# LayerNorm statistics moved off GpSimd, and its transposes placed later, in a two-layer decoder trunk

## The chip, the cores and the metric

The kernel runs on one core of one Trainium2 chip. The metric is the device time of one execution in microseconds (us). Three runs of the kernel before took 904.04, 904.43 and 904.75 us; their median is 904.43 us. The profile comes from a further execution that took 903.08 us.

## The reference

The program is a decoder trunk of two layers over 256 tokens of width 1024, in float32. Each layer has three sublayers: a mixer (three kinds of attention, gated and projected), a cross-attention into a memory of 256 tokens, and a squared-ReLU MLP of width 4096. Behind each stands the update that the change touches:

```python
def layer_norm(x, g, b):
    mu = jnp.mean(x32, axis=-1, keepdims=True)
    var = jnp.mean(jnp.square(x32 - mu), axis=-1, keepdims=True)
    return ((x32 - mu) * lax.rsqrt(var + LN_EPS) * g + b).astype(x.dtype)
...
for l in range(DEPTH):
    y = hybrid_mixer(x, ...)
    x = layer_norm(DN_ALPHA * x + y, ln_g[l, 0], ln_b[l, 0])
    y = memory_cross_attention(x, mem, ...)
    x = layer_norm(DN_ALPHA * x + y, ln_g[l, 1], ln_b[l, 1])
    y = jnp.square(jax.nn.relu(x @ mlp_w_up[l])) @ mlp_w_down[l]
    x = layer_norm(DN_ALPHA * x + y, ln_g[l, 2], ln_b[l, 2])
return x
```

So there are six LayerNorms, each over 256 tokens.

## The kernel before, in words

The 256 tokens are two halves of 128, one token per partition; the residual stream is kept in `xtok` (128 x 2 x 1024). Each LayerNorm is therefore done twice, once per half (`tb` 0 and 1): twelve LayerNorm halves in all. The text names them by place and half: M0 and M1 behind the mixer, X0 and X1 behind the cross-attention, F0 and F1 behind the MLP. In the second layer F0 and F1 end the program and write the output.

Every product is done in three passes, because each float32 operand is split into a high and a low part that TensorE takes at full speed: high times high, high times low, low times high (`mm3`, L322). ScalarE makes the high part of a weight piece (`whi`, or `phi` where it lies in a page; L266) and VectorE the low part (`wlo`, `plo`; L267), in pieces of 128 x 512. The same two engines split the activations: `xhi` (L340) and `xlo` (L341) are the residual stream, transposed, with the channels on the partitions. Weights come from one stream in HBM through a ring of five raw buffers; SyncE issues the load of a buffer once VectorE has taken its last piece from it.

A LayerNorm half works on two column halves. `ln_part` (L450, VectorE) adds the sublayer's product to the residual and sums each row into `mv[:, 0]` or `mv[:, 1]`. `ln_square` (L461, ScalarE) squares the columns, with a bias made of the first sum, and puts the row sums into `mv[:, 2]` and `mv[:, 3]`. The rest are one-column operations (128 x 1) on `mv`: three scaled copies of the first sum (L459), the eps (L463), and in `stats` the mean's remainder (L475), its square (L476), the variance (L477) and the power -0.5 (L478), all on GpSimd, and the mean on VectorE (L479). Two passes of VectorE then make the result: z = (x - mean) * g (L482, tile `lnz`) and x = z * rstd + b (L486). Where a sublayer follows, TensorE transposes the new x in four 128 x 128 pieces per column half (L492) and the two splits follow.

Two things set the order. `Side` queues hold small steps that are put between the big products: a step is issued when so many ticks (about one us of TensorE work each) have gone by, or at once where its result is needed (`need`). For LayerNorm these are `stats`, at once, and `result` twice, one tick apart; `LNW` is the wait of the first. The tile framework then schedules the program on each engine by its own estimates, so that the order on an engine is not simply the order of the code. Each engine takes its instructions strictly in that order.

Of the kernel before, what the change touches and what calls it, by code (L numbers as in the profile page):

```python
# [10 lines left out]
F32 = mybir.dt.float32  # L11
F32R = mybir.dt.float32r
AF = mybir.ActivationFunctionType
OP = mybir.AluOpType
# [4 lines left out]
D = 1024  # L19
L = 2  # L20
P = 128
# [4 lines left out]
ROOT = 32.0  # L26
# [5 lines left out]
WN = 2.0  # L32
WF = 1.5
WARM = 10
LNW = 1
NP = 8
TICK = 1.0
AHEAD = 4
# [191 lines left out]
class Kernel:  # L230
# [223 lines left out]
    def ln_square(self, tb, i):  # L454
        nc, mv = self.nc, self.mv[tb]
        xs = self.xtok[:, tb, 512 * i:512 * i + 512]
        if i == 0:
            for c, k in ((4, -2.0 / (D * ROOT)), (5, 1.0 / D), (6, -1.0 / D)):
                nc.gpsimd.tensor_scalar(mv[:, c:c + 1], mv[:, 0:1], k, None, op0=OP.mult)  # L459
        sq = self.half([P, 512], F32, "lnsq")  # L460
        nc.scalar.activation(sq, xs, AF.Square, bias=mv[:, 4:5], scale=1.0 / ROOT, accum_out=mv[:, 2 + i:3 + i])  # L461
        if i == 0:
            nc.gpsimd.tensor_scalar(mv[:, 7:8], mv[:, 2:3], 1e-5, None, op0=OP.add)  # L463

    def layer_norm(self, tb, gb, final=False):

        nc = self.nc
        x, mv = self.xtok[:, tb, :], self.mv[tb]
        col = [mv[:, i:i + 1] for i in range(12)]
        st = {}  # L470

        def stats():
            z = st["z"] = self.page([P, D], F32, "lnz")

            nc.gpsimd.tensor_scalar(col[8], col[1], -1.0 / D, col[5], op0=OP.mult, op1=OP.add)  # L475
            nc.gpsimd.tensor_scalar(col[9], col[8], col[8], col[7], op0=OP.mult, op1=OP.subtract)  # L476
            nc.gpsimd.tensor_tensor(col[10], col[3], col[9], op=OP.subtract)  # L477
            nc.gpsimd.tensor_tensor(col[11], col[10], self.mhalf, op=OP.pow)  # L478
            nc.vector.tensor_scalar(col[6], col[1], -1.0 / D, col[6], op0=OP.mult, op1=OP.add)  # L479
            for i in range(2):  # L480
                c = slice(512 * i, 512 * i + 512)
                nc.vector.scalar_tensor_tensor(z[:, c], x[:, c], col[6], gb[0][:, c], op0=OP.add, op1=OP.mult)  # L482

        def result(i):
            c = slice(512 * i, 512 * i + 512)
            nc.vector.scalar_tensor_tensor(x[:, c], st["z"][:, c], col[11], gb[1][:, c], op0=OP.mult, op1=OP.add)  # L486
            if final:
                nc.sync.dma_start(self.out[tb * P:(tb + 1) * P, c], x[:, c])
                return
            ps = self.bank("T", [P, 4, P])  # L490
            for k in range(4):
                nc.tensor.transpose(ps[:, k, :], x[:, 512 * i + k * P:512 * i + (k + 1) * P], self.ident)  # L492
            ds = (slice(None), slice(4 * i, 4 * i + 4), slice(tb * P, (tb + 1) * P))
            self.to_hilo(self.xhi[ds], self.xlo[ds], ps)
        tag = ("ln", tb)
        self.side[1].add(stats, 0, tag)
        self.side[1].add(lambda: result(0), LNW, tag)
        self.side[1].add(lambda: result(1), 1, tag)
        self.side[1].tick()

    def ln_done(self, tb):
# [679 lines left out]
```

## Time and profile before

| | |
|---|---|
| median of 3 runs | 904.43 us (904.04 to 904.75) |
| the profiled execution | 903.08 us |
| its span (first to last instruction) | 901.3 us |
| TensorE matmul busy | 877.9 us, 97% of the span, 6034 instructions |
| VectorE busy | 643.7 us, 71% |
| ScalarE busy | 540.9 us, 60% |
| GpSimd busy | 52.8 us, 6%, 114 instructions |
| granted TensorE clock | 0.997 over the span, the 2.4 GHz level |

The 1.8 us between the execution's time and its span lie before the first and behind the last instruction. Names of engines in the rows: PE is TensorE's matmul, PEld its weight load, DVE is VectorE, ACT is ScalarE, POOL is GpSimd, SP is SyncE. `out<-in` names the tiles written and read; a bracket behind a row gives the time for which the engine sat idle before it, and the instruction that ended this.

### The profile page before, as it was taken

The numbers are of one execution on the slowest core, as the hardware profiler recorded it, in microseconds if no ns is written. First come the engines' busy times: TensorE is split into PE (matmuls) and PEld (weight loads), VectorE is DVE, ScalarE is ACT, GpSimd is POOL, SyncE is SP. The second block draws the span as 40 slices with busy tenths as digits, with TensorE's granted clock in tenths as the row PEclk, the third lists the DMA queues.
The fourth block names the chain that finished last, engine by engine and source line by source line (L and its number), as shares of the span: only waits on it lengthen the run. The fifth ranks groups of instructions, "written<-read, shape, count | busy, mean of one in ns | idle before, by whom it ended". The sixth has DMA issues, their size and how long they took to land.

```text
span 901.3 us, 16105 instructions
## 1 busy us (share of the span) xinstructions
PE 877.9 (97%) x6034; PEld 798.0 (89%) x6034; DVE 643.7 (71%) x1411; ACT 540.9 (60%) x1173; POOL 52.8 (6%) x114
## 2 busy tenths in 40 slices
PE   8999999999999999999999999999999999999996
PEld 6999899998877999999889999999988689999994
DVE  5888898768886555555776989886778845555554
ACT  6777967556683444555656777675567545555551
POOL 1000000001211000000130000000021300000002
PEclk9999999999999999999999999999999999999998
DMA  9854645547553566666645435554667446666631
GB/s 330 264 184 146 207 159 158 160 148 275 181 201 118 187 194 192 190 188 190 209 123 179 143 118 178 178 160 139 194 210 252 165 123 187 190 196 188 191 95 47
DMA packets 46539, 160.80 MB, mean 178 GB/s; under 512 B 5941, under 2 KB 7381, under 8 KB 46334
## 3 DMA queue, kind: packets, MB, share of 16 engines
q1 hardware_dynamic: 46462, 159.78, 55.2%
q8 instruction: 47, 0.77, 0.3%
q14 instruction: 30, 0.25, 0.1%
HBM read 158.68 MB, written 1.07 MB: 177 GB/s over the span
## 4 chain that ended last, share of the span: by engine, by line
PE 86%; DVE 5%; POOL 3%; ACT 2%; issue 2%; DMA 1%; DVEq 0%; SPq 0%; POOLq 0%
PE mm L322 51%; PE S L322 14%; PE O L322 10%; DVE wlo L267 1%; PE S L744 1%; PE T L927 1%; POOL mv L476 1%; PE S L1050 1%; DVE xtok L450 1%; DVE xtok L486 1%; PE T L551 1%; PE O L561 1%; DVE xlo L341 1%; PE T L492 1%; DMA raw<-in_wst_dram 1%
## 5 line engine op out<-in xcount | busy, mean ns | idle before, releaser
L267 DVE TENSOR_TENSOR wlo<-raw,whi 128x512 fp32r<-128x512 f32 x524 | 341.0, 687 | 114.1 <-ACT whi L266 110.5
L266 ACT ACTIVATE whi<-raw 128x512 fp32r<-128x512 f32 x524 | 302.2, 624 | 145.1 <-issue 89.3
L322 PE MATMUL mm<-xhi,whi 128*128 128x256 f32 x1024 | 143.9, 282 | 0.1
L322 PE MATMUL mm<-xlo,whi 128*128 128x256 f32 x1024 | 143.8, 281 | 0.0
L322 PE MATMUL mm<-xhi,wlo 128*128 128x256 f32 x1024 | 142.7, 281 | 0.0
L322 PEld LDWEIGHTS mm<-xhi,whi 128*128 128x128 f32 x1024 | 131.8, 188 | 3.7 <-issue 0.7
L322 PEld LDWEIGHTS mm<-xhi,wlo 128*128 128x128 f32 x1024 | 130.4, 188 | 1.6 <-issue 0.3
L322 PEld LDWEIGHTS mm<-xlo,whi 128*128 128x128 f32 x1024 | 130.8, 188 | 1.1
L512 ACT ACTIVATE P<-sb,nm 128x128 f32<-128x128 f32 (+1 forms) x96 | 42.7, 445 | 16.5 <-DVE nm L510 16.1
L322 PE MATMUL S<-whi,hh 128*128 128x512 f32 x128 | 50.4, 394 | 0.0
L322 PE MATMUL S<-wlo,hh 128*128 128x512 f32 x128 | 50.1, 391 | 0.0
L322 PE MATMUL O<-whi,hh 128*128 128x512 f32 x128 | 50.0, 391 | 0.0
L322 PE MATMUL O<-wlo,hh 128*128 128x512 f32 x128 | 49.9, 390 | 0.0
L322 PE MATMUL O<-whi,hl 128*128 128x512 f32 x128 | 49.8, 389 | 0.0
L322 PE MATMUL S<-whi,hl 128*128 128x512 f32 x128 | 49.7, 389 | 0.0
L459 POOL TENSOR_SCALAR mv<-mv 128x1 f32<-128x1 f32 x36 | 9.0, 264 | 672.7 <-DVE xtok L450 671.7
L1125 DVE TENSOR_TENSOR tg<-tg 128x512 f32<-128x512 f32 x28 | 19.4, 692 | 38.4 <-ACT tg L1124 38.4
L1124 ACT ACTIVATE tg<-mm 128x512 f32<-128x512 f32 x28 | 16.7, 597 | 43.2 <-PE mm L322 43.2
L461 ACT ACTIVATE lnsq<-xtok,mv 128x512 f32<-128x512 f32 x24 | 17.3, 721 | 28.5 <-POOL mv L459 15.8
L267 DVE TENSOR_TENSOR plo<-raw,phi 128x512 fp32r<-128x512 f32 x40 | 26.0, 689 | 5.1 <-ACT phi L266 5.0
L322 PEld LDWEIGHTS S<-wlo,hh 128*128 128x128 f32 x128 | 24.0, 188 | 5.6
L322 PEld LDWEIGHTS O<-whi,hl 128*128 128x128 f32 x128 | 24.0, 188 | 5.1
(306 smaller groups left out, 1437.0 us busy)
## 6 DMA issues: line engine op xcount, KB each, us to landing
raw<-in_wst_dram SPq DMA_DIRECT2D x281, 512.0 KB, 3.9
lng<-in_lng_dram SPq DMA_DIRECT2D x6, 512.0 KB, 5.9
lnb<-in_lnb_dram SPq DMA_DIRECT2D x6, 512.0 KB, 5.8
wskew<-bias_scratch SPq DMA_DIRECT2D x4, 400.0 KB, 5.7
xt<-in_xT_dram SPq DMA_DIRECT2D x4, 256.0 KB, 4.1
xtok<-in_xtok_dram SPq DMA_DIRECT2D x1, 1024.0 KB, 6.8
out_dram<-xtok SPq DMA_DIRECT2D x4, 256.0 KB
raw<-in_wst_dram SPq DMA_DIRECT2D x2, 256.0 KB, 4.3
```

What stands on the lines that cost most here:

```text
L266: self.nc.scalar.activation(hi[sl], self.raws[u][sl], AF.Copy)
L267: self.nc.vector.tensor_sub(lo[sl], self.raws[u][sl], r(hi[sl]))
L322: mm(out, a[i], b[j], start=first and ps == 0 and k == 0, stop=last and ps == 2 and k == n - 1)
L341: nc.vector.tensor_sub(lo, src, r(hi))
L450: nc.vector.scalar_tensor_tensor(xs, xs, ALPHA, ac, op0=OP.mult, op1=OP.add, accum_out=mv[:, i:i + 1])
L461: nc.scalar.activation(sq, xs, AF.Square, bias=mv[:, 4:5], scale=1.0 / ROOT, accum_out=mv[:, 2 + i:3 + i])
L476: nc.gpsimd.tensor_scalar(col[9], col[8], col[8], col[7], op0=OP.mult, op1=OP.subtract)
L486: nc.vector.scalar_tensor_tensor(x[:, c], st["z"][:, c], col[11], gb[1][:, c], op0=OP.mult, op1=OP.add)
L492: nc.tensor.transpose(ps[:, k, :], x[:, 512 * i + k * P:512 * i + (k + 1) * P], self.ident)
L512: nc.scalar.activation(p_ap, t[:, :n], AF.Exp, bias=nmax, scale=-1.0, accum_out=sums)
L1124: nc.scalar.activation(t, ps, AF.Relu)
L1125: nc.vector.tensor_mul(t, t, t)
```

## The change

The one-column statistics leave GpSimd, except the power. ScalarE now makes the bias of the square (column 4) and adds the eps (column 7) with two activations in `ln_square`, and the variance (column 10) with a third in `stats`. VectorE makes the two mean columns (5 and 8) straight from both sums, and the square of the mean (9). Per LayerNorm half seven of eight GpSimd operations go, three ScalarE operations come, and VectorE has three one-column operations in place of one.

The transposes become a step of their own, `turn`. The two passes for x are now issued inside `stats`, behind the two passes for z, and `turn(0)` waits three ticks (`LNW` 3 instead of 1), `turn(1)` one more.

```diff
-LNW = 1
+LNW = 3
...
         if i == 0:
-            for c, k in ((4, -2.0 / (D * ROOT)), (5, 1.0 / D), (6, -1.0 / D)):
-                nc.gpsimd.tensor_scalar(mv[:, c:c + 1], mv[:, 0:1], k, None, op0=OP.mult)
+            nc.scalar.activation(mv[:, 4:5], mv[:, 0:1], AF.Copy, scale=-2.0 / (D * ROOT))
         sq = self.half([P, 512], F32, "lnsq")
         nc.scalar.activation(sq, xs, AF.Square, bias=mv[:, 4:5], scale=1.0 / ROOT, accum_out=mv[:, 2 + i:3 + i])
         if i == 0:
-            nc.gpsimd.tensor_scalar(mv[:, 7:8], mv[:, 2:3], 1e-5, None, op0=OP.add)
+            nc.scalar.activation(mv[:, 7:8], mv[:, 2:3], AF.Copy, bias=1e-5)
...
+        def scaled(i):
+            c = slice(512 * i, 512 * i + 512)
+            nc.vector.scalar_tensor_tensor(st["z"][:, c], x[:, c], col[5], gb[0][:, c], op0=OP.add, op1=OP.mult)
+
         def stats():
-            z = st["z"] = self.page([P, D], F32, "lnz")
-
-            nc.gpsimd.tensor_scalar(col[8], col[1], -1.0 / D, col[5], op0=OP.mult, op1=OP.add)
-            nc.gpsimd.tensor_scalar(col[9], col[8], col[8], col[7], op0=OP.mult, op1=OP.subtract)
-            nc.gpsimd.tensor_tensor(col[10], col[3], col[9], op=OP.subtract)
+            st["z"] = self.page([P, D], F32, "lnz")
+
+            nc.vector.tensor_scalar(col[5], col[1], col[0], -1.0 / D, op0=OP.add, op1=OP.mult)
+            nc.vector.tensor_scalar(col[8], col[1], col[0], -1.0 / D, op0=OP.subtract, op1=OP.mult)
+            nc.vector.tensor_scalar(col[9], col[8], col[8], col[7], op0=OP.mult, op1=OP.subtract)
+            nc.scalar.activation(col[10], col[9], AF.Identity, bias=col[3], scale=-1.0)
             nc.gpsimd.tensor_tensor(col[11], col[10], self.mhalf, op=OP.pow)
-            nc.vector.tensor_scalar(col[6], col[1], -1.0 / D, col[6], op0=OP.mult, op1=OP.add)
             for i in range(2):
-                c = slice(512 * i, 512 * i + 512)
-                nc.vector.scalar_tensor_tensor(z[:, c], x[:, c], col[6], gb[0][:, c], op0=OP.add, op1=OP.mult)
+                scaled(i)
+            for i in range(2):
+                result(i)
...
-                return
+
+        def turn(i):
             ps = self.bank("T", [P, 4, P])
...
         self.side[1].add(stats, 0, tag)
-        self.side[1].add(lambda: result(0), LNW, tag)
-        self.side[1].add(lambda: result(1), 1, tag)
+        if not final:
+            self.side[1].add(lambda: turn(0), LNW, tag)
+            self.side[1].add(lambda: turn(1), 1, tag)
```

On TensorE, in the first layer, from the second weight unit of the MLP's first product for half 0 (`mm_3539` before, `mm_3533` in the changed kernel) to the first matmul for half 1 (`mm_3540`, `mm_3534`). The transposes (`T`, L492) are those of X1; `phi` and `plo` are the weights, `xhi` and `xlo` the residual stream. Before:

```order
L322 MATMUL mm_3539<-phi_3326,xhi_92 128x512 x2
L322 MATMUL mm_3539<-phi_3326,xlo_93 128x512 x2
L322 MATMUL mm_3539<-plo_3327,xhi_92 128x512 x2
L322 MATMUL mm_3539<-phi_3434,xhi_92 128x512 x2
L322 MATMUL mm_3539<-phi_3434,xlo_93 128x512 x2
L322 MATMUL mm_3539<-plo_3435,xhi_92 128x512 x2
L322 MATMUL mm_3539<-phi_3494,xhi_92 128x512 x2
L322 MATMUL mm_3539<-phi_3494,xlo_93 128x512 x2
L322 MATMUL mm_3539<-plo_3495,xhi_92 128x512 x2
L492 MATMUL T_3550<-cst_151,xtok_1255 128x128 x4
L492 MATMUL T_3568<-cst_151,xtok_1255 128x128 x4
L322 MATMUL mm_3540<-phi_3291,xhi_92 128x512 x2
```

The same stretch of TensorE in the changed kernel, where the transposes are L497:

```order
L322 MATMUL mm_3533<-phi_3430,xhi_92 128x512 x2
L322 MATMUL mm_3533<-phi_3430,xlo_93 128x512 x2
L322 MATMUL mm_3533<-plo_3431,xhi_92 128x512 x2
L322 MATMUL mm_3533<-phi_3482,xhi_92 128x512
L497 MATMUL T_3561<-cst_151,xtok_1255 128x128 x4
L322 MATMUL mm_3533<-phi_3482,xhi_92 128x512
L497 MATMUL T_3576<-cst_151,xtok_1255 128x128 x4
L322 MATMUL mm_3533<-phi_3482,xlo_93 128x512 x2
L322 MATMUL mm_3533<-plo_3483,xhi_92 128x512 x2
L322 MATMUL mm_3534<-phi_3287,xhi_92 128x512 x2
```

Here the transposes have moved ahead: five of the 24 matmuls for half 0 stand behind the first four transposes and four behind all eight; before, all eight stood behind the 24.

On VectorE, at the same place, from X0's second result (in the changed kernel both results) to the results of X1; the number behind a name is that of its buffer: `lnz` is z, `lnb` and `lng` the LayerNorm's b and g, `mv` the statistics. Before:

```order
L486 SCALAR_TENSOR_TENSOR xtok_1255<-lnz_3474,mv_3442,lnb_3397 128x512
L267 TENSOR_TENSOR plo_3495<-raw_3205,phi_3494 128x512
L341 TENSOR_TENSOR xlo_93<-T_3487,xhi_92 128x4x128
L450 SCALAR_TENSOR_TENSOR xtok_1255,mv_3517<-xtok_1255,S_3482 128x512
L341 TENSOR_TENSOR xlo_93<-T_3504,xhi_92 128x4x128
L450 SCALAR_TENSOR_TENSOR xtok_1255,mv_3517<-xtok_1255,S_3483 128x512
L267 TENSOR_TENSOR wlo_3683<-raw_3513,whi_3682 128x512
L479 TENSOR_SCALAR mv_3517<-mv_3517 128x1
L267 TENSOR_TENSOR wlo_3683<-raw_3513,whi_3682 128x512
L482 SCALAR_TENSOR_TENSOR lnz_3531<-xtok_1255,mv_3517,lng_3395 128x512 x2
L486 SCALAR_TENSOR_TENSOR xtok_1255<-lnz_3531,mv_3517,lnb_3397 128x512 x2
```

The same in the changed kernel, where z is L473 and the result L490:

```order
L490 SCALAR_TENSOR_TENSOR xtok_1255<-lnz_3468,mv_3438,lnb_3393 128x512 x2
L267 TENSOR_TENSOR plo_3483<-raw_3201,phi_3482 128x512
L450 SCALAR_TENSOR_TENSOR xtok_1255,mv_3497<-xtok_1255,S_3478 128x512
L341 TENSOR_TENSOR xlo_93<-T_3506,xhi_92 128x4x128
L450 SCALAR_TENSOR_TENSOR xtok_1255,mv_3497<-xtok_1255,S_3479 128x512
L341 TENSOR_TENSOR xlo_93<-T_3516,xhi_92 128x4x128
L478 TENSOR_SCALAR mv_3497<-mv_3497 128x1
L479 TENSOR_SCALAR mv_3497<-mv_3497 128x1
L473 SCALAR_TENSOR_TENSOR lnz_3523<-xtok_1255,mv_3497,lng_3391 128x512
L480 TENSOR_SCALAR mv_3497<-mv_3497 128x1
L473 SCALAR_TENSOR_TENSOR lnz_3523<-xtok_1255,mv_3497,lng_3391 128x512
L490 SCALAR_TENSOR_TENSOR xtok_1255<-lnz_3523,mv_3497,lnb_3393 128x512 x2
```

The sums of the next half (L450) now each stand one place ahead of a split (`xlo`) where they stood behind it, the two `wlo` splits that stood around the statistics are gone from there, and one of the three one-column operations stands between the two passes for z.

On ScalarE, behind the square of M1's second column half, in the first layer. Before:

```order
L461 ACTIVATE lnsq_3090,mv_2972<-xtok_1255,mv_2972 128x512
L266 ACTIVATE whi_3191<-raw_3014 128x512 x2
L266 ACTIVATE phi_3291<-raw_3075 128x512 x2
L340 ACTIVATE xhi_92<-T_3111 128x4x128
L340 ACTIVATE xhi_92<-T_3131 128x4x128
L1028 ACTIVATE kx_3100<-mm_3101 128x512
```

And in the changed kernel, where L481 is the variance (column 10):

```order
L460 ACTIVATE lnsq_3086,mv_2970<-xtok_1255,mv_2970 128x512
L266 ACTIVATE whi_3187<-raw_3010 128x512 x2
L481 ACTIVATE mv_2970<-mv_2970 128x1
L266 ACTIVATE phi_3287<-raw_3064 128x512 x2
L340 ACTIVATE xhi_92<-T_3132 128x4x128
L1034 ACTIVATE kx_3098<-mm_3099 128x512
L340 ACTIVATE xhi_92<-T_3151 128x4x128
```

The variance stands in ScalarE's queue behind two weight splits.

## Rows read from the trace of the kernel before

**Rows 1.** The page: busy time of TensorE, and the chain that ended last, by engine.

```profile
PE 877.9 (97%) x6034; PEld 798.0 (89%) x6034; DVE 643.7 (71%) x1411; ACT 540.9 (60%) x1173; POOL 52.8 (6%) x114
PE 86%; DVE 5%; POOL 3%; ACT 2%; issue 2%; DMA 1%; DVEq 0%; SPq 0%; POOLq 0%
```

**Rows 2.** What TensorE waited for over the whole span (us in total, times, longest), longest first.

```profile
PE T L492 <- DVE xtok L486: 9.1, 10, 1.4
PE S L322 <- ACT xhi L340: 1.2, 2, 0.7
```

**Rows 3.** All instructions on the statistics tile `mv`, by line: durations in ns (shortest/median/longest), first and last start in us.

```profile
L459 POOL TENSOR_SCALAR mv<-mv x36: 202/208/713, 217.5 to 893.4; 128x1 f32<-128x1 f32 x36
...
L475 POOL TENSOR_SCALAR mv<-mv x12: 261/442/1262, 224.1 to 894.8; 128x1 f32<-128x1 f32 x12
L476 POOL TENSOR_SCALAR mv<-mv x12: 377/1037/1903, 224.5 to 895.5; 128x1 f32<-128x1 f32 x12
...
L478 POOL TENSOR_TENSOR mv<-mv,mhalf x12: 564/568/575, 226.5 to 896.3; 128x1 f32<-128x1 f32 x12
```

**Rows 4.** The timeline at X0 and X1 of the first layer: start us, us, engine, line, operation.

```profile
261.55 0.08 DVE L450 DVE_READ_ACCUMULATOR xtok<-xtok,mm 128x1 f32 x1
...
264.54 0.75 DVE L486 SCALAR_TENSOR_TENSOR xtok<-lnz,mv,lnb 128x512 f32<-128x512 f32 x1 [0.73 <-POOL mv L478]
...
265.44 0.63 PE L492 MATMUL T<-cst,xtok 128*128 128x128 f32 x4 [0.57 <-DVE xtok L486]
...
265.82 0.71 PE L322 MATMUL S<-whi,oxh 128*128 128x512 f32 x2
...
267.07 0.69 DVE L341 TENSOR_TENSOR xlo<-T,xhi 128x512 fp32r<-128x512 f32 x1
...
267.81 0.73 PE L322 MATMUL mm<-phi,xlo 128*128 128x512 f32 x2
...
269.56 0.08 DVE L450 DVE_READ_ACCUMULATOR xtok<-xtok,S 128x1 f32 x1
...
270.43 1.26 POOL L475 TENSOR_SCALAR mv<-mv 128x1 f32<-128x1 f32 x1
...
270.89 1.41 DVE L482 SCALAR_TENSOR_TENSOR lnz<-xtok,mv,lng 128x512 f32<-128x512 f32 x2
...
273.51 1.42 DVE L486 SCALAR_TENSOR_TENSOR xtok<-lnz,mv,lnb 128x512 f32<-128x512 f32 x2 [1.21 <-POOL mv L478]
...
274.41 1.29 PE L492 MATMUL T<-cst,xtok 128*128 128x128 f32 x8 [1.20 <-DVE xtok L486]
...
275.72 0.73 PE L322 MATMUL mm<-phi,xhi 128*128 128x512 f32 x2
```

**Rows 5.** The timeline at the second layer's start: a power on GpSimd (L609, two columns) beside a pair of VectorE splits, and again with VectorE idle.

```profile
460.64 1.29 DVE L267 TENSOR_TENSOR wlo<-raw,whi 128x512 fp32r<-128x512 f32 x2
...
460.82 1.07 POOL L609 TENSOR_TENSOR rs<-ss,mhalf 128x2 f32<-128x2 f32 x1 [4.08 <-DVE ss L608]
...
466.71 0.69 POOL L609 TENSOR_TENSOR rs<-ss,mhalf 128x2 f32<-128x2 f32 x1 [4.83 <-DVE ss L608]
```

**Rows 6.** ScalarE's groups by line and form (count, busy us, mean ns of one), the nearest to a one-column activation, without and with a bias read from a column.

```profile
L837 ACT ACTIVATE kb<-T 128x16 fp32r<-128x16 f32 x4 | 0.7, 171 | 0.0
...
L607 ACT ACTIVATE sq<-S 128x128 f32<-128x128 f32 x4 | 1.1, 272 | 0.0
```

**Rows 7.** The timeline at M0, M1 and in the cross-attention behind them, first layer.

```profile
227.87 0.66 PE L492 MATMUL T<-cst,xtok 128*128 128x128 f32 x4 [0.81 <-DVE xtok L486]
...
233.55 1.15 ACT L266 ACTIVATE whi<-raw 128x512 fp32r<-128x512 f32 x2 [0.61 <-ACT lnsq L461]
...
235.79 1.41 DVE L486 SCALAR_TENSOR_TENSOR xtok<-lnz,mv,lnb 128x512 f32<-128x512 f32 x2 [1.05 <-POOL mv L478]
...
236.68 0.63 PE L492 MATMUL T<-cst,xtok 128*128 128x128 f32 x4 [0.94 <-DVE xtok L486]
...
247.48 1.15 ACT L266 ACTIVATE whi<-raw 128x512 fp32r<-128x512 f32 x2 [0.75 <-DMA raw<-in_wst_dram]
...
248.54 0.46 ACT L537 ACTIVATE P<-S,nm 128x256 f32<-128x256 f32 x1
...
250.18 0.41 PEld L551 LDWEIGHTS T<-cst,P 128*128 128x128 f32 x3 [0.24 <-DVE P L546]
```

**Rows 8.** The chain of waits in order of time: a piece of 24 matmuls of 512 columns without a gap (start us, us).

```profile
438.61 5.46 PE S L322 x24
```

**Rows 9.** The timeline at F0 and F1 of the first layer.

```profile
444.70 0.08 DVE L450 DVE_READ_ACCUMULATOR xtok<-xtok,S 128x1 f32 x1
...
444.89 0.21 DVE L479 TENSOR_SCALAR mv<-mv 128x1 f32<-128x1 f32 x1
...
448.57 0.66 PE L492 MATMUL T<-cst,xtok 128*128 128x128 f32 x4 [1.35 <-DVE xtok L486]
...
452.72 0.08 DVE L450 DVE_READ_ACCUMULATOR xtok<-xtok,O 128x1 f32 x1
...
457.67 1.29 PE L492 MATMUL T<-cst,xtok 128*128 128x128 f32 x8 [0.78 <-DVE xtok L486]
```

**Rows 10.** The timeline of the last LayerNorm half, F1 of the second layer.

```profile
893.36 0.08 DVE L450 DVE_READ_ACCUMULATOR xtok<-xtok,O 128x1 f32 x1
...
896.86 1.41 DVE L486 SCALAR_TENSOR_TENSOR xtok<-lnz,mv,lnb 128x512 f32<-128x512 f32 x2 [1.57 <-POOL mv L478]
```

## The prediction

> **What bounds the kernel now.** I read the page first. TensorE's matmuls are busy 97% of the span, and the chain that ended last is 86% TensorE, 5% VectorE and 3% GpSimd [rows 1]. So only what makes TensorE wait, and the tail behind its last matmul, can give time back. Next come TensorE's waits. One line is far ahead: the LayerNorm transposes (L492) wait for the result pass (L486), 9.1 us in ten waits, the longest 1.4 us [rows 2]. Ten, because of the twelve LayerNorm halves the last two have no transposes. Then the statistics, by line: the square of the mean (L476) takes 0.38 to 1.90 us, its forerunner (L475) 0.26 to 1.26 us, the power (L478) always 0.57 us [rows 3]. The long ones run beside VectorE's two-input passes: at X1, L475 takes 1.26 us while L482 runs [rows 4]. Last, the timeline at each place, for the chain from the second sum to the transposes. The waits are 0.81 us at M0 and 0.94 at M1 [rows 7], 0.57 at X0 and 1.20 at X1 [rows 4], 1.35 at F0 and 0.78 at F1 [rows 9]. M and X occur in both layers, so 2 x 3.52 + 2.13 = 9.2 us, which is the line's sum. The bound on what the transposes can give is thus about 9 us, 1%.
>
> **The chain itself.** Count from the end of the read of the second sum to the start of the first result. Before it is 273.51 - 269.64 = 3.87 us at X1 and 264.54 - 261.63 = 2.91 at X0 [rows 4], and 896.86 - 893.44 = 3.42 in the last half [rows 10]. In the changed kernel VectorE starts 0.11 us behind the read (444.89 - 444.78) and a one-column operation takes 0.21 us [rows 9]; a z pass takes 1.41 / 2 = 0.71 [rows 4]. Its order is columns 5 and 8, z, column 9, z: 0.11 + 3 x 0.21 + 2 x 0.71 + 0.04 = 2.20 us to the end of z. ScalarE makes column 10 behind column 9, at about 1.5. No row has a one-column activation; the nearest take 0.17 us (16 columns) and 0.27 (128 columns) [rows 6], so I take 0.3 us with its wait for column 10 and 0.2 for the others. The power then arrives at 1.9, while the second z runs until 2.2. The one power that met VectorE's two-input passes took 1.07 us instead of 0.69: it came 0.18 us into the first of two (0.65 us each) and ended as if begun when that one ended [rows 5]. So the power runs behind z, 0.57 us, and the result begins at 2.20 + 0.57 + 0.04 = 2.8 us. If VectorE doesn't keep it out, the result begins at 2.25; if the pass behind z keeps it out as well, at 3.4 to 3.5.
>
> The Trainium skill, page "SBUF — State Buffer", section "Who interferes with whom", says that a VectorE instruction with two SBUF inputs and a GpSimd instruction that reads SBUF exclude each other, and that the first to start keeps the shared ports for its whole length. Its first half agrees with rows 5. Its second half, that a started power holds up VectorE, no row shows: the splits beside the power take 1.29 us as a pair, 0.65 each. What this would do here is a rival below.
>
> **The tail.** In the last half nothing stands between z and the results: 3.42 - 2.8 = 0.6 us sooner, and everything behind follows. Bounds: 0 (power kept out longer) and 1.2 (not kept out).
>
> **X0 and X1, twice.** At X0, VectorE has two small low parts of the attention output in front of column 9, worth 0.45 us, so z ends at 261.63 + 2.2 + 0.45 = 264.3 and the result starts at 264.9, 0.35 later than before [rows 4]. TensorE has three matmuls more in front, 3 x 0.23 (24 take 5.46 us [rows 8]) = 0.7, so it hardly waits. But the split `xlo` that it needs next now stands behind both results (0.67 each), one weight split (0.60) and the first sum of X1 (0.69): 264.9 + 1.34 + 0.60 + 0.69 = 267.5 where it was 267.07. So the first matmul on `xlo` moves from 267.81 [rows 4] to 268.25, a loss of 0.45. The second sum of X1 follows at once and ends at 267.5 + 0.6 + 0.7 = 268.8, where it was 269.64: the second `xlo` and one weight split have moved out of its way. Behind that `xlo` (0.6) the chain starts at 269.4 and gives the result at 269.4 + 2.8 = 272.2, the transposes 0.9 behind it as now (274.41 - 273.51), at 273.1 instead of 274.41. TensorE gets there after 17 matmuls, 268.25 + 3.9 = 272.15, and waits 0.95. Two groups of four transposes (0.38 each, 265.82 - 265.44), one matmul between them and four behind: 273.1 + 0.76 + 1.15 = 275.0 for the first matmul of half 1, which was at 275.72. A gain of 0.7 us per layer. Bounds: 0 (another 0.65 on the power, twice) and 1.8 (X's two waits).
>
> **F0 and F1, once.** At F0 the transposes come 448.57 - 444.78 = 3.8 us behind the second sum [rows 9] and would come 2.8 + 0.9 = 3.7 behind it, with one more matmul in front: 0.1 + 0.23 = 0.3. At F1 the second sum comes 0.3 sooner, at 452.5; a weight split stands in front of column 5 as it does now (0.6), another behind z but under the power: transposes at 452.5 + 0.6 + 3.7 = 456.8 instead of 457.67. TensorE was there at 457.67 - 0.78 = 456.89; 0.3 earlier and with two more matmuls in front, it is there at 457.05 and finds them ready: the 0.78 us go. It then waits some 0.3 for `xhi`, which now is needed right behind the transposes. Sum 0.3 + 0.78 - 0.3 = 0.8. Bounds 0.1 and 2.1.
>
> **M0 and M1, twice.** Taken alone, one and four to six matmuls more in front and the shorter chain would give up to 0.7 us per layer. I cost it at nothing: TensorE soon comes to attention transposes that wait for a probability, whose exponential (248.54) stands on ScalarE behind a weight split that itself waited for its DMA until 247.48; TensorE waited only 0.24 there [rows 7]. A lead becomes waiting, and these transposes stand two matmuls earlier now. Bounds: -0.25 and 0.7.
>
> **What costs nothing.** GpSimd's removed operations are off the chain except as above. 36 activations of 0.2 to 0.3 us, some 9 us, go onto ScalarE (60% busy) and 24 operations of 0.21 us, 5 us, onto VectorE (71%) [rows 1]; both idle around the LayerNorms (1.21 us before the results at X1 [rows 4]). If that cover goes, the price is the slower rival's. Order and number of SyncE's DMAs stay.
>
> **Sum.** 0.6 + 2 x 0.7 + 0.8 + 0 = 2.8 us. The profiled execution of 903.08 becomes 900.3; against the median, which is 1.35 above it, 904.4 - 2.8 = 901.6 us. With all low bounds it would be 904.8, with all high ones 904.4 - (1.2 + 3.6 + 2.1 + 1.4) = 896.1.
>
> **The rivals.** (a) A started power holds VectorE's next two-input pass until it is done, as the skill's page has it. A weight split stands between z and the results at M0, M1, X0 and F1, so there the result comes behind the power and that split, 0.6 later: X falls from 0.7 to 0.1, F from 0.8 to 0.3. Gain 0.6 + 0.2 + 0.3 = 1.1, time 903.3. For it: GpSimd gets its turn when a pass ends. Against it: the 1.29 us of rows 5.
> (b) Every lead of TensorE is eaten downstream as behind M1, and only the tail stays: 904.4 - 0.6 = 903.8. For it: `xlo` at X0 and `xhi` at F1. Against it: there are no large waits of TensorE outside the LayerNorms [rows 2].
> (c) Slower: the statistics queue on ScalarE, where GpSimd stood idle for them. At M1 column 10 stands behind two weight splits that end at 234.70 [rows 7]; then 235.0 for column 10, 235.6 for the split on VectorE to end, 236.2 for the power: the result at 236.25 where it was 235.79, 0.45 late. Should the same happen wherever a split stands in front of column 10 (M0, M1, X0, twice, F0, F1), it is 8 x 0.45 - 0.6 = 3.0 us: 907.4. It decides if those splits wait for their raw data or buffer, as the 0.61 us before those at M1 hint; against it, elsewhere column 9 comes later than the split.
> (d) The results are ready everywhere when TensorE comes: 904.4 - 9.1 - 0.6 = 894.7. Against it: at X1 the transposes moved forward.
>
> **How the numbers follow.** Forecast 0.48, (a) 0.17, (b) 0.14, (c) 0.13, (d) 0.08. The likeliest's own range is 899.8 to 903.4. About 0.2%, 1.8 us, can be told from no change: faster is below 902.6, slower above 906.2. Faster: 0.82 of the forecast, 0.25 of (a), all of (d): 0.39 + 0.04 + 0.08 = 0.51. Slower: most of (c), 0.11. The rest, 0.38, is within. The range from 898.5 to 905.2 leaves out (d) and most of (c).
>
> **What would show it.** Right: TensorE's wait for L490 at the transposes falls from 9.1 to about 5 us, with X1 near 0.95 and F1 near 0; the power takes more than 0.57 us where z or a split runs; the results begin 2.8 us behind the second sum; the first matmul of the MLP's half 1 comes 0.7 us sooner, counted from the end of the output projection's last matmul; the cross-attention's transposes behind M1 wait longer than 0.24. Wrong: L481 idle behind a weight split, a split stretched by the power, or `xlo` waits of more than half a microsecond. The forecast falls if the wait of the transposes stays at 9 us.

## The result: 5.5 us, twice the forecast, and the profile after

The changed kernel takes 897.9 us (median of 6 runs, 896.1 to 898.6), the kernel before 904.2 us beside it (6 runs). The ratio is 0.9939, with a 95% interval of 0.9927 to 0.9950: 5.5 us less, between 4.5 and 6.6. The profiled execution has a span of 896.7 us where it was 901.3. The forecast said faster, by 2.8 us, at 901.6, with a range from 898.5 to 905.2. The 897.9 us lie 0.6 below that range; but the forecast was counted from 904.43 us, and 0.9939 of that is 898.9, just inside it.

The page of the changed kernel, busy time and chain, answers to [rows 1]:

```profile
PE 879.3 (98%) x6034; PEld 799.1 (89%) x6034; DVE 647.5 (72%) x1435; ACT 546.7 (61%) x1209; POOL 18.2 (2%) x30
PE 84%; DVE 5%; ACT 4%; DMA 4%; issue 2%; POOL 1%; DVEq 0%; POOLq 0%; SPq 0%; ACTq 0%
```

GpSimd gave up 34.6 us of work, and ScalarE and VectorE took 5.8 and 3.8 us of it. Its share of the chain that ended last fell from 3% to 1%; that of the DMAs rose from 1% to 4%. TensorE's waits, which answer to [rows 2]:

```profile
PE T L497 <- DVE xtok L490: 2.7, 7, 0.5
...
PE mm L322 <- ACT oxh L340: 0.8, 2, 0.6
PE mm L322 <- DVE xlo L341: 0.7, 2, 0.3
...
PE T L557 <- DVE P L552: 0.3, 1, 0.3
```

The transposes waited 9.1 us in ten waits and now wait 2.7 in seven. That is 6.4 us, of which some went to other waits, which were not there before: for the low parts in front of `mm`, for the attention's output and for a probability.

To see where the time came out, I cut the span at matmuls that both kernels have. The projection's stretch (X), for one, runs from its first matmul to the first of the MLP's second product (`S<-whi,hh`; the texts below call it the MLP's first); in the kernel before:

```profile
262.32 1.18 PE L322 MATMUL S<-whi,oxh 128*128 128x512 f32 x3 [0.34 <-ACT oxh L340]
...
288.23 0.40 PE L322 MATMUL S<-whi,hh 128*128 128x512 f32 x1
```

and in the changed one:

```profile
262.50 1.14 PE L322 MATMUL S<-whi,oxh 128*128 128x512 f32 x3 [0.31 <-ACT oxh L340]
...
287.24 0.39 PE L322 MATMUL S<-whi,hh 128*128 128x512 f32 x1
```

25.91 us became 24.74. All stretches, in us, each the difference of two such starts, the last up to the end of the last instruction ("T" is the first transpose; M begins with the mixer's output projection, the first matmul `S<-whi,mg`):

| stretch | before, layers 1 and 2 | after | gain | forecast |
|---|---|---|---|---|
| M0, M1 and cross-attention | 55.62, 55.62 | 55.36, 55.38 | 0.26, 0.24 | 0, 0 |
| X0, X1, projection | 25.91, 25.92 | 24.74, 24.72 | 1.17, 1.20 | 0.7, 0.7 |
| MLP's second product to T at F1 | 169.43 | 168.21 | 1.22 | 0.8 (both rows of F) |
| T at F1 to the next M | 192.24 | 192.40 | -0.16 | |
| last matmul to the end | 8.96 | 7.86 | 1.10 | 0.6 |

One cut is not at the same work: two more matmuls (0.46 us) stand in front of T at F1 in the changed kernel, as the forecast had it. Counted at the same work, the two F rows are a gain of 1.68 and a loss of 0.62.

The rest of layer 2 is the same (160.86 us). The gains sum to 5.03; the changed execution reached the first M 0.44 us later, before any edited instruction, which leaves the 4.6 us between the spans.

What the statistics cost now, by line on tile `mv`, answers to [rows 3] (ns: shortest, median, longest):

```profile
L478 DVE TENSOR_SCALAR mv<-mv x12: 202/214/215, 224.4 to 890.0; 128x1 f32<-128x1 f32 x12
L479 DVE TENSOR_SCALAR mv<-mv x12: 201/204/206, 224.6 to 890.1; 128x1 f32<-128x1 f32 x12
L480 DVE TENSOR_SCALAR mv<-mv x12: 265/269/274, 225.3 to 890.9; 128x1 f32<-128x1 f32 x12
L481 ACT ACTIVATE mv<-mv x12: 276/294/297, 225.7 to 891.2; 128x1 f32<-128x1 f32 x12
L482 POOL TENSOR_TENSOR mv<-mv,mhalf x12: 538/682/1203, 226.1 to 891.7; 128x1 f32<-128x1 f32 x12
```

On VectorE and ScalarE shortest and longest lie within 8%, where L475 and L476 went up to 1.26 and 1.90 us. Only the power, left on GpSimd, is now stretched, to as much as 1.20 us where it always took 0.57. The last half, which answers to [rows 10]:

```profile
889.85 0.08 DVE L450 DVE_READ_ACCUMULATOR xtok<-xtok,O 128x1 f32 x1
889.97 0.21 DVE L478 TENSOR_SCALAR mv<-mv 128x1 f32<-128x1 f32 x1
...
890.10 0.20 DVE L479 TENSOR_SCALAR mv<-mv 128x1 f32<-128x1 f32 x1
...
890.22 0.75 DVE L473 SCALAR_TENSOR_TENSOR lnz<-xtok,mv,lng 128x512 f32<-128x512 f32 x1
...
890.88 0.27 DVE L480 TENSOR_SCALAR mv<-mv 128x1 f32<-128x1 f32 x1
891.07 0.74 DVE L473 SCALAR_TENSOR_TENSOR lnz<-xtok,mv,lng 128x512 f32<-128x512 f32 x1
891.25 0.29 ACT L481 ACTIVATE mv<-mv 128x1 f32<-128x1 f32 x1 [0.32 <-DVE mv L480]
891.68 0.54 POOL L482 TENSOR_TENSOR mv<-mv,mhalf 128x1 f32<-128x1 f32 x1 [4.90 <-ACT mv L481]
892.26 1.42 DVE L490 SCALAR_TENSOR_TENSOR xtok<-lnz,mv,lnb 128x512 f32<-128x512 f32 x2 [0.45 <-POOL mv L482]
```

From the end of the read (889.93) to the first result is 2.33 us, where it was 3.42. The chain did not shrink by as much everywhere. Counted in the same way, it went from 3.12 to 2.93 at M0, 3.70 to 3.41 at M1, 3.86 to 2.81 at X1, 2.98 to 2.33 at F0 and 3.97 to 3.42 at F1 of the first layer; at X0 it grew, from 2.91 to 3.31. And the second column half at X, which answers to the later rows of [rows 4]:

```profile
267.70 0.68 DVE L341 TENSOR_TENSOR xlo<-T,xhi 128x512 fp32r<-128x512 f32 x1
...
268.30 0.68 DVE L450 SCALAR_TENSOR_TENSOR xtok<-xtok,S 128x512 f32<-128x512 f32 x1
268.44 0.73 PE L322 MATMUL mm<-phi,xlo 128*128 128x512 f32 x2 [0.33 <-DVE xlo L341]
...
268.90 0.68 DVE L341 TENSOR_TENSOR xlo<-T,xhi 128x512 fp32r<-128x512 f32 x1
...
269.50 0.20 DVE L478 TENSOR_SCALAR mv<-mv 128x1 f32<-128x1 f32 x1
...
271.79 1.42 DVE L490 SCALAR_TENSOR_TENSOR xtok<-lnz,mv,lnb 128x512 f32<-128x512 f32 x2 [0.45 <-POOL mv L482]
...
272.69 0.63 PE L497 MATMUL T<-cst,xtok 128*128 128x128 f32 x4
```

The transposes at X1 have no wait behind them any more. VectorE's order is sum, low part, sum, low part, then the columns, and from the first column to the result it takes 271.79 - 269.50 = 2.29 us, as in the last half (892.26 - 889.97).

### The profile page after: what moved, and what is told of

Read it like the earlier page. It is cut to its first block, busy times and chain, and to the rows that moved or that the text cites. A ratio compares the mean times of both kernels' runs of the same rounds, so it can differ in the third digit from the quotient of the medians.

```text
span 896.7 us, 16065 instructions
## 1 busy us (share of the span) xinstructions
PE 879.3 (98%) x6034; PEld 799.1 (89%) x6034; DVE 647.5 (72%) x1435; ACT 546.7 (61%) x1209; POOL 18.2 (2%) x30
## 4 chain that ended last, share of the span: by engine, by line
PE 84%; DVE 5%; ACT 4%; DMA 4%; issue 2%; POOL 1%; DVEq 0%; POOLq 0%; SPq 0%; ACTq 0%
PE mm L322 51%; PE S L322 14%; PE O L322 11%; DMA raw<-in_wst_dram 3%; DVE wlo L267 2%; ACT whi L266 1%; PE S L750 1%; PE T L933 1%; DVE xtok L490 1%; POOL mv L482 1%; DVE xtok L450 1%; PE T L497 1%; PE T L557 1%; ACT lnsq L460 1%; PE O L945 1%
## 5 line engine op out<-in xcount | busy, mean ns | idle before, releaser
L322 PEld LDWEIGHTS O<-wlo,hh 128*128 128x128 f32 x128 | 24.0, 188 | 5.1
L322 PEld LDWEIGHTS O<-whi,hh 128*128 128x128 f32 x128 | 24.0, 188 | 5.0
```

The lines of the kernel that those rows point to most:

```text
L322: mm(out, a[i], b[j], start=first and ps == 0 and k == 0, stop=last and ps == 2 and k == n - 1)
```

## The experiments

Eleven runs in three sets, each set on one chip with its own runs of the kernel before (medians 902.7, 903.0 and 902.5 us). The theory: TensorE and the tail pay for the time between the second sum and the result, the statistics shorten it, and the order adds what it makes ready in time. The rivals: the order alone does it; or it is the count of operations that left GpSimd.

**The statistics alone.** Each result pass and its transposes issued as one step, as before.

```diff
-LNW = 3
+LNW = 1
...
-            for i in range(2):
-                result(i)
...
-            self.side[1].add(lambda: turn(0), LNW, tag)
+        self.side[1].add(lambda: result(0), LNW, tag)
...
```

> The new statistics on ScalarE and VectorE, but each result pass and its transposes issued in one step, in the order of the kernel before. Theory (the shorter chain is what pays, and the order adds the rest): the chain from the second sum to the first result is as short as in the changed kernel, 2.3 to 2.4 us in the last half, so the tail's 1.1 us come whole; with the shorter chain in front of the transposes, X0+X1 give 0.5 to 1.2 us per layer and F0+F1 0.5 to 1.0; some 3 to 4.5 us below the kernel before, 899.7 to 901.2. Rival (the order does it): only the tail's 1.1 us, 903.1. Rival (the order does nothing): all of it, 897.9 to 898.5.

Measured: 898.5 us, ratio 0.9951 (0.9934 to 0.9968), 4.4 us below, at the upper end of the 3 to 4.5 (its absolute times were counted from a slower run of the kernel before). All chains are as in the changed kernel, to 0.01 us. Tail 7.85, T at F1 after 168.21, as in the changed kernel; X is 25.29 in both layers, about half of its gain.

**The order alone.** GpSimd's statistics with the new order.

```diff
-LNW = 1
+LNW = 3
...
+            for i in range(2):
+                result(i)
...
+        def turn(i):
```

> The statistics of the kernel before on GpSimd, but both result passes right behind z and the transposes later, as in the changed kernel. Theory: the tail gives nothing (the chain in the last half stays 3.4 us); the transposes stand behind more matmuls, so their wait falls by 0.2 to 0.7 us each, but at X1 VectorE waits for the power with everything behind it; between 0.5 us slower and 1.5 us faster than before, 902.7 to 904.7. Rival (the order does it): 4 us or more below, 900.2 or less.

Measured: 901.9 us, ratio 0.9990 (0.9979 to 1.0000), 0.9 us below. Tail 8.97, F 169.30, X 25.36, but M and cross-attention 55.92 in layer 2, 0.3 slower. So the rival that the order alone does it falls: 4.4 and 0.9 us make up 5.3 of the 5.5.

**A second power in the chain.**

```diff
+            nc.gpsimd.tensor_tensor(col[6], col[10], self.mhalf, op=OP.pow)
             nc.gpsimd.tensor_tensor(col[11], col[10], self.mhalf, op=OP.pow)
```

> The changed kernel with a second power of the same kind issued on GpSimd in front of the one that is used, so that each chain is one power longer. Theory (the chain's length is what TensorE and the tail pay for): each chain is 0.55 us longer; the tail pays it whole, X0, X1, M0, M1 and F0 pay most of it, F1 little: 3 to 5 us above the changed kernel, 901 to 903. Rival (TensorE now has slack at the transposes): only the tail's 0.55 us, 898.4. Rival (VectorE's passes keep the power out, as the prediction had it): the second power is held until the pass behind ends and costs 0.7 to 1.1 instead of 0.55, 6 us or more above.

Measured: 903.0 us, ratio 0.9995 (0.9985 to 1.0005): against the changed kernel's 0.9939 that is 0.0056 x 903 = 5.1 us. At X1, F0 and in the last half the second power starts 0.50 us behind the first, and the chains are 0.5 us longer (0.69 in the last half). The tail pays 0.78, X 1.0 per layer, M and cross-attention 0.7 and 0.85, F 1.0: most chains are paid whole, two to a stretch, M not quite. There is no slack at these transposes: a term of 0.5 us per chain is 5 us of the kernel.

**Transposes that need no result.**

```diff
-                nc.tensor.transpose(ps[:, k, :], x[:, 512 * i + k * P:512 * i + (k + 1) * P], self.ident)
+                nc.tensor.transpose(ps[:, k, :], st["z"][:, 512 * i + k * P:512 * i + (k + 1) * P], self.ident)
```

> The changed kernel with the LayerNorm transposes reading z (the scaled and centred rows) instead of the finished result: they no longer wait for the power and the result pass, and the output is another. It leaves out the last step of the normalisation for everything that goes through the transposes. Theory (what is left of the waits can still be had, but for M0 and M1, where attention downstream takes part of it): the transposes' wait falls from 7.0 us to under 2, the time by 3 to 5 us, to 893 to 895. Rival (every lead is eaten downstream): less than 1 us, 897 or more. Rival (d, all waits turn into time): 6 to 7 us, 891 to 892.

The expectation misread the view: seven is the number of the waits that were left, 2.7 us their sum, so its 3 to 7 us could not be had. Measured: 895.8 us, ratio 0.9917 (0.9900 to 0.9934), 2.0 us below the changed kernel. The transposes' wait falls from 2.7 to 0.8 us, but waits for low parts (1.7, where it was 0.7) and for the cross-attention's probability (1.6, where it was 0.3) take their place:

```profile
PE mm L322 <- DVE xlo L341: 1.7, 2, 0.8
PE T L557 <- DVE P L552: 1.6, 2, 0.8
...
PE T L497 <- DVE lnz L473: 0.8, 2, 0.4
```

**The changed kernel again.**

> The changed kernel again, unedited, so that the three next to it stand against it on one chip: 0.9939 of the kernel before, about 5.5 us below it. In its trace the groups of eight 256-column matmuls of the second layer's mixer should show whether their pace (0.94 or 0.91 us a group) belongs to the kernel or to the execution: if to the execution, it may differ from the first profile's 0.94.

Measured: 896.8 us, ratio 0.9929 (0.9910 to 0.9949). X is 24.72 and 24.74, F 168.21, tail 7.86, to within 0.02 of the first profile, but M and cross-attention are 54.91 and 55.44, and T at F1 to the next M 191.95 in place of 192.40. Behind the first profile's F1 a group of eight matmuls takes 0.94 us:

```profile
468.77 1.10 PE L322 MATMUL mm<-xlo,whi 128*128 128x256 f32 x8
469.72 1.10 PE L322 MATMUL mm<-xhi,whi 128*128 128x256 f32 x8
```

In the repeat the same groups start 0.90 to 0.91 us apart (468.05, 468.95). The pace belongs to the execution, and over this stretch it is worth 0.45 us. The M row differs for another reason. In layer 1 of the first profile the attention's output (`oxh`) stands on ScalarE behind a weight split that waited for its DMA, and TensorE comes to it 0.43 us later than in the repeat, where that split did not wait:

```profile
256.03 1.15 ACT L266 ACTIVATE whi<-raw 128x512 fp32r<-128x512 f32 x2 [0.87 <-DMA raw<-in_wst_dram]
...
257.40 0.97 PE L322 MATMUL mm<-whi,oxh 128*128 128x512 f32 x3 [0.16 <-ACT oxh L340]
```

So the M row and the second F row of the table above are not sure to within some 0.45 us; the X, first F and tail rows are.

**Column 9 ahead of both z passes.**

```diff
-            nc.vector.tensor_scalar(col[5], col[1], col[0], -1.0 / D, op0=OP.add, op1=OP.mult)
...
+            nc.vector.scalar_tensor_tensor(col[6], col[9], 0.0, col[1], op0=OP.mult, op1=OP.add)
+            nc.vector.tensor_scalar(col[5], col[6], col[0], -1.0 / D, op0=OP.add, op1=OP.mult)
```

> The changed kernel with columns 8 and 9 ahead of both z passes on VectorE (the mean's column is made to depend on column 9 by a term that adds zero, one operation more). Theory (the chain's length is what is paid): column 10 and the power no longer stand behind z's first pass, and the result follows z's second pass at once; the chain of the last half falls from 2.33 to about 2.1 us, the tail by 0.2, each of X0, X1, M0, M1 and F0 by 0.1 to 0.3 where the first square is ready in time; 0.5 to 1.5 us below the changed kernel. Rival (z waits for the first square, which the two sums close behind each other make late): 0 to 1 us above it.

Measured: 903.5 us, ratio 1.0005 (0.9995 to 1.0015): 6 to 7 us above the changed kernel, outside both expectations. X is 26.52, F 170.24, the tail 8.03. In the halves with nothing in between, the four columns start 0.32, 0.31 and 0.19 us apart and z 0.25 behind the last, as each waits for the one before. Worse, VectorE's order fills the gaps between them with weight splits; at X1:

```profile
271.33 0.68 DVE L267 TENSOR_TENSOR wlo<-raw,whi 128x512 fp32r<-128x512 f32 x1
...
271.93 0.15 DVE L480 SCALAR_TENSOR_TENSOR mv<-mv 128x1 f32<-128x1 f32 x1
...
272.00 0.68 DVE L267 TENSOR_TENSOR wlo<-raw,whi 128x512 fp32r<-128x512 f32 x1
272.60 0.20 DVE L481 TENSOR_SCALAR mv<-mv 128x1 f32<-128x1 f32 x1
272.73 0.68 DVE L267 TENSOR_TENSOR wlo<-raw,whi 128x512 fp32r<-128x512 f32 x1
273.32 1.41 DVE L473 SCALAR_TENSOR_TENSOR lnz<-xtok,mv,lng 128x512 f32<-128x512 f32 x2
```

Here z begins 2.9 us behind the first column (270.43), where it began 0.25 behind it. In the changed kernel the first z pass covers the step from column 8 to column 9.

**Column 10 back on GpSimd.**

```diff
-            nc.scalar.activation(col[10], col[9], AF.Identity, bias=col[3], scale=-1.0)
+            nc.gpsimd.tensor_tensor(col[10], col[3], col[9], op=OP.subtract)
```

> The changed kernel with one of its moves undone: column 10 (one subtraction of two columns) is made on GpSimd again, in front of the power, and not on ScalarE; everything else stays. Theory (what cost was GpSimd's small operations held by VectorE's two-input passes): the subtraction falls beside z's second pass and ends only with it, 0.5 to 0.75 us instead of 0.19, and the power behind it, so each chain is 0.2 to 0.6 us longer and the time 1.5 to 4 us above the changed kernel. Rival (what cost was the number of operations and crossings): one crossing between engines less, 0.1 to 0.3 us shorter per chain, 0.5 to 1.5 us below it.

Measured: 899.1 us, ratio 0.9954 (0.9938 to 0.9971), 2.3 us above the changed kernel in the same set (the two intervals overlap by a little). At X1:

```profile
270.69 0.74 DVE L473 SCALAR_TENSOR_TENSOR lnz<-xtok,mv,lng 128x512 f32<-128x512 f32 x1
...
270.92 0.56 POOL L481 TENSOR_TENSOR mv<-mv 128x1 f32<-128x1 f32 x1 [6.31 <-DVE mv L480]
...
271.56 0.55 POOL L482 TENSOR_TENSOR mv<-mv,mhalf 128x1 f32<-128x1 f32 x1
...
272.14 1.41 DVE L490 SCALAR_TENSOR_TENSOR xtok<-lnz,mv,lnb 128x512 f32<-128x512 f32 x2 [0.71 <-POOL mv L482]
```

The subtraction ends 0.05 us behind the z pass (271.43), as the theory had it, and from the first column it is 272.14 - 269.60 = 2.54 us, 0.25 longer; M0, F0 and the last half are longer by as much. At M1, X0 and the first layer's F1 the chain is 0.33 us shorter, which the theory did not have: there the power, which a weight split held in the changed kernel, follows the subtraction and takes its 0.54 to 0.56. X loses 0.53 per layer and the tail 0.27. The other 0.25 at X come from X0: its result was sooner, and both weight splits then stood behind it, in front of the sums. By X and the tail the move is worth 1.3 us, by the ratios 2.3.

**The transposes due five, two and four ticks behind the statistics** instead of three; the edit for five (the others put 2 and 4 there):

```diff
-LNW = 3
+LNW = 5
```

> The changed kernel with the transposes due later still (five ticks behind the statistics instead of three, one number). Theory (at three the transposes at X1 and F1 find their result ready and the others wait 0.3 to 0.5 us; further back only moves the wait to the splits behind them): the wait of the transposes falls from 2.7 to under 1.5 us, within 0.8 us of the changed kernel. Rival (the later the better): 1.5 us or more below. Rival (TensorE runs out of other matmuls and the splits come late): 1 us or more above.

> The changed kernel with the transposes due two ticks behind the statistics instead of three (one number). By the written order only the second half of the output projection changes: its eight transposes come in one piece, two matmuls later than now, with two matmuls of the MLP in front of the last of the projection, as in the run with the statistics alone. Theory (the 0.57 us per layer that the changed order was worth in that stretch come from where these transposes stand, and from nothing else): the stretch from the projection's first matmul to the MLP's first falls back from 24.73 to 25.3 us in both layers, everything else stays: 1.1 us above the changed kernel. Rival (they come from the results standing together on VectorE): 24.7, no difference.

> The changed kernel with the transposes due four ticks behind the statistics instead of three (one number). Theory (a lead at the transposes is worth something only while the splits behind them and the attention's transposes are not later still): M0's and F0's transposes stand two or three matmuls later and wait less, but the first matmuls on their high and low parts wait instead, and the projection's stretch is 25.3 to 25.6 us as with five ticks: 1 to 3 us above the changed kernel. Rival (a step between a good and a bad point): 0.5 us or more below it.

Measured: 900.3 us, 0.9960 (0.9946 to 0.9973), for five; 898.4, 0.9952 (0.9940 to 0.9964), for two; 899.2, 0.9960 (0.9948 to 0.9972), for four. All are slower than three by their ratios; the intervals overlap with those of three by a little, but X tells them apart: 25.64, 25.31 and 25.64, where three had 24.7. So five ticks missed its 0.8 us, and its last case came, 1 us or more above. With five ticks the transposes wait less, and others more:

```profile
PE T L557 <- DVE P L552: 2.8, 2, 1.8
PE mm L322 <- DVE xlo L341: 1.9, 2, 0.9
...
PE T L497 <- DVE xtok L490: 1.3, 4, 0.4
```

With the new statistics as they are, X has one of three values by VectorE's order at X1. Sum, low part, sum, low part, with three ticks: 24.7. Sum, both low parts, sum, with one or two: 25.3. Both sums, both low parts, with four or five: 25.6, as TensorE then waits 0.95 for the first low part. With two ticks the number was as the theory had it, yet the place of the transposes is not the whole cause: the second sum stands behind the second low part, its read ends 0.6 us later (268.96 - 261.89 = 7.07 behind the projection's first matmul, and 268.98 - 262.50 = 6.48 with three ticks), and all that follows is late by that.

**Only the columns around the first square back on GpSimd.**

```diff
-            nc.scalar.activation(mv[:, 4:5], mv[:, 0:1], AF.Copy, scale=-2.0 / (D * ROOT))
+            nc.gpsimd.tensor_scalar(mv[:, 4:5], mv[:, 0:1], -2.0 / (D * ROOT), None, op0=OP.mult)
...
-            nc.scalar.activation(mv[:, 7:8], mv[:, 2:3], AF.Copy, bias=1e-5)
+            nc.gpsimd.tensor_scalar(mv[:, 7:8], mv[:, 2:3], 1e-5, None, op0=OP.add)
```

> The changed kernel with another of its moves undone alone: the two columns around the first square (4 and 7) are made on GpSimd again, where columns 5, 8, 9 and 10 stay on VectorE and ScalarE; TensorE's order is the same. Theory (only what stands between the second sum and the result is paid): both columns lie behind the first sum, early enough in the last half and at F0, so the tail stays at 7.9 us; only at X1, M1 and F1, where the two sums follow each other closely and a two-input pass runs beside them, do they come late, by 0.2 to 0.6 us: 0 to 1.5 us above the changed kernel. Rival (each operation that leaves GpSimd brings its share): a third of the gain goes, 2 us or more above it.

Measured: 897.6 us, ratio 0.9943 (0.9931 to 0.9955). X is 24.83, 0.1 above; F 168.23, tail 7.88, the same. By X and the tail these two of GpSimd's operations were worth 0.2 us, by the ratios 0.4 to 1.3; the one between column 9 and the power was worth 1.3 and 2.3. What counts is which of them the result waits for.

## Why the prediction was right in direction and half in size

**What bounded it** was right: TensorE's wait for the result, and the tail. It named 9.1 us as the most the transposes can give; 3.9 of the 5.03 us came from there, and 1.1 from the tail.

**The step that failed is the chain of 2.8 us**, and it failed in two terms. First the end of z. The prediction put the columns at their durations, 0.21 us each, behind one another, and the first 0.11 behind the read: 2.20 us. In the trace the first starts 0.04 behind the read, the second 0.13 behind the first (889.97, 890.10), and they overlap; z ends at 891.81, 1.88 behind the read. Then the power. The prediction let it wait for z and run its whole 0.57 us behind it. It began 0.13 before z's end (891.68), took 0.54, no more than a power takes with nothing beside it, and ended 0.41 behind z (892.22 - 891.81). With 0.04 to the result that is 2.33 and not 2.8: 0.3 from the columns and their start, 0.16 from the power.

So z did not hold the power in the last half; nor did it at F0 and X1, where the power takes 0.54 too. Of the prediction's three cases the time lies nearest to the one without a hold. (That case's 2.25 us counts only to z's end; by the prediction's own terms it is 1.9 + 0.57 + 0.04 = 2.5.) What holds the power elsewhere is the weight split behind z, as in the third case. M0:

```profile
225.52 0.74 DVE L473 SCALAR_TENSOR_TENSOR lnz<-xtok,mv,lng 128x512 f32<-128x512 f32 x1
...
226.14 1.14 POOL L482 TENSOR_TENSOR mv<-mv,mhalf 128x1 f32<-128x1 f32 x1 [125.59 <-ACT mv L481]
...
226.19 0.68 DVE L267 TENSOR_TENSOR wlo<-raw,whi 128x512 fp32r<-128x512 f32 x1
...
227.32 1.41 DVE L490 SCALAR_TENSOR_TENSOR xtok<-lnz,mv,lnb 128x512 f32<-128x512 f32 x2 [0.45 <-POOL mv L482]
```

The split ends at 226.87 and the power at 227.28, 0.41 later. In all twelve LayerNorm halves the power ends 0.39 to 0.41 us behind the last two-input pass that began no later than 0.11 us into it. A z pass can hold it as well, when the power comes earlier: in the run with column 9 ahead, F0's power began 0.21 us into the first z pass and took 0.94 us.

**The tail** was 0.6 and is 1.10: the missing 0.5 is the chain's.

**X0 and X1** were followed almost step by step, in part by luck. X0's result was forecast 264.9 - 262.32 = 2.58 us behind the projection's first matmul and came at 265.16 - 262.50 = 2.66, but z ended 0.37 sooner than forecast (2.28 behind the read and not 2.65), and the split behind it, for which the forecast had no price, held the power, which took 0.87 us and not 0.57. The two errors cancel:

```profile
264.04 0.69 DVE L267 TENSOR_TENSOR plo<-raw,phi 128x512 fp32r<-128x512 f32 x1
...
264.26 0.87 POOL L482 TENSOR_TENSOR mv<-mv,mhalf 128x1 f32<-128x1 f32 x1 [28.54 <-ACT mv L481]
...
265.16 1.41 DVE L490 SCALAR_TENSOR_TENSOR xtok<-lnz,mv,lnb 128x512 f32<-128x512 f32 x2 [0.43 <-POOL mv L482]
```

Counted from the projection's first matmul, the first low-part matmul was forecast at 268.25 - 262.32 = 5.93 and came at 268.44 - 262.50 = 5.94; the end of X1's second sum at 6.48 and came at 6.48; the chain's start at 7.08 and came at 7.00. Then the result was forecast at 9.88 and came at 9.29. TensorE's wait of 0.95 went with it. The gain is 1.2 and not 0.7: again the chain's 0.5. The order's part was not in the forecast as such: the three values of X show that the sum between the two low parts, which the prediction took as given, is worth 0.6 of the 1.2 per layer.

**F0 and F1**: F1's wait went whole, as forecast. At F0 the transposes' wait fell from 1.35 to 0.47, by 0.88 where the forecast's terms make 0.3: again the chain's 0.5. So the gain up to the same matmul is 1.68 and not 1.08. Behind it 0.62 is lost, where 0.3 was forecast. The forecast's wait for `xhi` is not there; a wait of 0.46 us of the mixer's transposes for `ccn` on ScalarE is, which the kernel before did not have, and the rest lies within the pace of the executions.

**M0 and M1** were costed at nothing, because a lead would become waiting behind them. Much of it did: the transposes wait 0.95 us less per layer (two waits of 0.40 in place of 0.81 and 0.94), the probability and the attention's output are waited for 0.5 to 0.6 more, and 0.25 came out. With five ticks the probability's wait grew to 1.8 us, so the mechanism is shown; how much it takes is not. It goes with the DMA wait shown above. Where that split waited 0.87 us or more (both layers of the first profile, layer 2 of the repeat), 0.17 to 0.26 came out; where it waited 0.4 or less (layer 1 of the repeat, both layers of the run with columns 4 and 7 on GpSimd, which has TensorE's same order), 0.41 to 0.93. The row at 247.48 in [rows 7] hinted at this; no run tests it.

**The rivals.** (a) A started power holds VectorE's next two-input pass: not seen. At M0 the split began 0.05 us behind the power and took its 0.68 us; the power was stretched instead. By the Trainium skill, page "SBUF — State Buffer", section "SBUF: two separate sides", whichever of the two starts first gets the shared ports for the whole instruction; by the starts that this trace records (226.14 and 226.19) it was not so. (b) Only the tail: fell, since X and F gave 3.4 us. (c) The statistics queue on ScalarE: at M1 column 10 did stand behind two weight splits, and the result still came 3.4 us behind the sum's read, where it had been 3.7; nothing was lost. (d) All waits vanish: not even the transposes without a result reached it.

## What to carry to other kernels

Where TensorE waits at nearly every hand-over, count the time from the last input to the first output in single operations, and move first what stands in that path beside a two-input VectorE pass; the same kind of operation off that path (columns 4 and 7) gave 0.2 us by the stretches. Add up starts, not durations, for short operations that don't depend on each other, and leave a long independent pass between those that do. When a due time decides the order, try the numbers beside it: two, four and five ticks lost 1 to 3 us, most of it at X, through the order on VectorE that came with them.

## What the runs showed of the hardware that was not expected

- A one-column VectorE operation (columns 5 and 8) takes 0.20 to 0.21 us, but the next independent one starts 0.12 to 0.13 us behind its start. One that needs its result starts 0.03 to 0.11 us behind its end, in the run with column 9 ahead 0.19 to 0.32 apart.
- A power on GpSimd (128 x 1) takes 0.54 to 0.57 us with nothing beside it, and the next one starts after 0.50. Beside a two-input VectorE pass it ends 0.4 us behind that pass, so 1.20 us at the worst here. With column 9 first, at M0, it slipped between two passes: it began 0.07 us before a split, ended 0.41 behind the z pass ahead of it, and neither was longer. What decides between this and 1.14 us stays open.
- At the start of the second layer's mixer, groups of eight 256-column matmuls run at 0.94 us in the first profile and at 0.91 in the repeat, with the same program and the same granted clock (1.00 over the stretch in both). What decides it stays open.
